# Two-layer HGRN2 + RWKV-7 trunk: 40 more projection products ahead of the inverse's corner products, gate tiles emptied by ScalarE alone, up-projection products over 128 rows

## The chip, the cores and the metric

The kernel runs on one core of one Trainium2 chip. The metric is the device time of one execution in microseconds (us), the median of three runs. One more execution was profiled; all rows of a trace below are of that one. Engines: PE is TensorE (PEld its weight loads), DVE is VectorE, ACT is ScalarE, POOL is GpSimd, SP issues most transfers.

## The reference

Two layers over a sequence of 512 with width 1024. In each layer:

```
h = x * (1 + scale) + shift            # shift, scale, gate from silu(c) @ w_ada + b_ada
P = h @ w_in                           # 49 column tiles of 128: q, f, i, z_hg | r, k, v, z_rw, w_down, a_down | g_hg, g_rw
o_hg = HGRN2(q, f, i), 4 heads of 128; normed, times silu(z_hg)
r, k, v, z_rw, w_down, a_down = token_shift(P_rw, mu)     # p + (previous token's p - p) * mu
decay from tanh(w_down) @ w_up + w0 ; a = sigmoid(a_down @ a_up + a0)
S_t = S_{t-1} (diag(w_t) - kk_t^T (a_t kk_t)) + v_t^T k_t ; y_t = S_t r_t   # RWKV-7, 8 heads of 64
y_rw = (groupnorm(y) + bonus) * silu(z_rw)
merged = sigmoid(g_hg) * (o_hg @ W_A) + sigmoid(g_rw) * (y_rw @ W_B)
x = LayerNorm(alpha * x + (1 + gate) * (merged @ w_out))
```

All is in float32.

## The kernel before

Activations lie transposed: 128 features on the partitions, 512 tokens along the free axis. A float32 product is made of three fast ones: `split` turns a weight tile into a high part (ACT copy, L120) and a low part (POOL subtraction, L125 `wl`), and `proj` (L252) multiplies high by high, high by low and low by high (L261, L262, L266). One column tile of `h @ w_in` is 24 such products of 128x512 into one PSUM tile `pj` (two of these exist), fed by two weight units of 12 products, each loaded by SP into one of three `raw` tiles and split into one of three `wh` and one of three `wl` tiles.

The recurrent part of a layer has long chains on DVE, so projection tiles serve as filling: a generator `fill` yields one product at a time, and `weave(main, fill, counts)` puts `counts[i]` of them on PE ahead of step i of `main`. Each engine works off its own queue in order, so a product that stands ahead of a step on PE is done before that step, and a step whose input is late holds everything behind it. The order of the other engines' queues comes from a scheduler that works at build time.

After the last head's preparation (p = 3) the filling is a chain of whole tiles (L1025): the merge gates `gate(j)` (two tiles each, in layer 0 one for j = 0; emptied by one ACT tanh a tile into buffers that stay until the output stage), then `zrw(p)`, then `zhg(p)`, then the other gates. A `zrw` tile ends in `rw_gate` (L666): the token shift is an ACT copy with a scale and a DVE instruction that reads PSUM (`shift`, L339: `u<-ppj,dvomm`, then L134 `u<-ppj,prm,u`), and silu is an ACT tanh and one more DVE instruction (L134 `z<-z,u`).

`rw_invert` (L501) inverts a triangular 64x64 block for each of 8 heads and 8 chunks. On DVE alone: four block transposes (L513), a substitution of many small multiplications (L125 `t<-t,t`) and sums (L521), four transposes back (L524), two more (L527). Then PE makes two sets of corner products of 32x32 (L535, copies L540 to SBUF; L549, copies L554). `WT` says how many filling products stand ahead of each quarter of these: 132 before the first, then 0, 13, 0, 14, 3, 0, 0. Ahead of them 35 (`WPR`) and 41 (`WHN`) products are taken from the same chain. Then come 8 chunks (`rw_chunk`, first instruction L577) with 24 filling products each (`WCH`), then `finish` with 65 (`WFI`), and `run(fill)` empties what is left of the chain: 57 products in layer 0 (552 in all) and 81 in layer 1 (576). Behind it come `gate_rows`, in layer 0 the `w_ada` columns of layer 1 (L302), and the branch and output projections.

`rw_wa` (L359) makes the up-projections: for each p and each of decay and a, one product over 128 rows (high weights by `x[i]`, whose halves hold the high and the low part of the activation) and one over 64 rows (low weights by the high half), L377 and L378, emptied by one ACT tanh. `wunit` splits their two weight tiles like all others. The tiles `x[i]` are of the tag `z` (four buffers), which the `w_ada` transfers of the next step need.

Of the kernel before, what the change touches and what calls it, by code (L numbers as in the profile page):

```python
# [12 lines left out]
F32 = mybir.dt.float32  # L13
F32R = mybir.dt.float32r
U8 = mybir.dt.uint8
AF = mybir.ActivationFunctionType
ALU = mybir.AluOpType
# [9 lines left out]
WHG = (0, 4, 16, 6, 11, 6, 6, 0, 8, 0, 6, 12)  # L27
WPR = (0, 4, 26, 5)
WHN = (0, 19, 0, 11, 11)
WT = (132, 0, 13, 0, 14, 3, 0, 0)  # L30
WCH = (0, 3, 3, 1, 7, 5, 5)
WNT = (0, 0, 2, 4, 0, 1, 0, 0)
WBO = (0, 31, 0, 23, 0, 18, 5, 50)
# [2 lines left out]
NP = 4  # L36
KT = 8
# [44 lines left out]
def body(ctx, tc, d):  # L82
    nc = tc.nc
    V, A, G, PE = nc.vector, nc.scalar, nc.gpsimd, nc.tensor
# [10 lines left out]
    def st(tag, shape, dt=F32):  # L95
        cnt[0] += 1
        return sp.tile(shape, dt, tag=tag, name=f"{tag}_{cnt[0]}", bufs=BUFS[tag])

    def ps(tag):
        cnt[0] += 1  # L100
        return pp.tile([128, 512], F32, tag=tag, name=f"p{tag}_{cnt[0]}", bufs=PB[tag])

    def u(shape=(128, 512), dt=F32):
        return st("u", list(shape), dt)
# [13 lines left out]
    def act(out, in_, f, scale=1.0, bias=0.0):  # L118
        if f == AF.Copy:
            A.activation(out, in_, f, scale=scale)  # L120
        else:
            A.activation(out, in_, f, scale=scale, bias=bias)  # L122

    def tt(e, o, a, b, op):
        e.tensor_tensor(o, a, b, op=op)  # L125
# [7 lines left out]
    def stt(o, a, s, b, op0, op1):  # L133
        V.scalar_tensor_tensor(o, a, s, b, op0=op0, op1=op1)  # L134
# [7 lines left out]
    mm = PE.matmul  # L142
# [54 lines left out]
    def P(n, l, i=None, w=None):  # L197
        o = PO[n, l]
        if i is not None:
            return prm[:, o + i:o + i + 1]  # L200
        return prm[:, o:o + w]

    dv = [dict() for _ in range(L)]
# [36 lines left out]
    def split(raw, hi, lo):  # L240
        act(hi, raw, AF.Copy)
        tt(G, lo, raw, hi.bitcast(F32), ALU.subtract)

    def wunit(src, th="wh", tl="wl"):
        raw = st("raw", [128, 512])
        nc.sync.dma_start(raw, src)
        hi = st(th, [128, 512], F32R)
        lo = st(tl, [128, 512], F32R)
        split(raw, hi, lo)
        return hi, lo  # L250
# [18 lines left out]
    def run(g):  # L269

        while True:
            try:
                next(g)
            except StopIteration as e:
                return e.value

    def weave(main, fill, counts, priority=0):


        last = None  # L280
        for i in itertools.count():
            for m in itertools.islice(fill, counts[i] if i < len(counts) else 0):
                last = m
            with ExitStack() as es:
                if priority:
                    es.enter_context(tc.high_priority(offset=priority))
                if last is not None:
                    es.enter_context(tc.issue_after(last.ins))
                if next(main, END) is END:
                    return  # L290
# [22 lines left out]
    def ada_next(*groups):  # L313

        for g, w in pend:
            ada_col(*g, w)
        pend[:] = []
        for l, n, k in groups:
            w = [st("z", [128, 512]) for _ in range(2)]
            for h in range(2):  # L320
                nc.sync.dma_start(w[h], d["w_ada"][l, n, k, :, h * 512:(h + 1) * 512])
            pend.append(((l, n, k), w))
# [16 lines left out]
    def shift(o, pst, l, c):  # L339
        act(o, pst, AF.Identity, scale=dv[l]["omm"][:, c:c + 1])  # L340
        stt(o[:, 1:], pst[:, :-1], P("mu", l, c), o[:, 1:], ALU.mult, ALU.add)
# [17 lines left out]
    def rw_wa(l, pst):  # L359

        wad = u()
        shift(wad, pst, l, 16)
        act(wad[0:64], wad[0:64], AF.Tanh)
        x = [st("z", [128, 512], F32R) for _ in range(2)]
        for i in range(2):
            r, q = slice(64 * i, 64 * i + 64), slice(64 - 64 * i, 128 - 64 * i)
            V.tensor_copy(x[i][r], wad[r])
            tt(V, x[i][q], wad[r], x[i][r].bitcast(F32), ALU.subtract)
        wu = [wunit(d["up"][l, i], *(("X", "X") if l else ("pu", "pu"))) for i in range(2)]
        rw["gt"], rw["vm"] = [], []  # L370
        for p in range(NP):
            cols = slice(p * 128, (p + 1) * 128)
            g = st("t4" if p < 3 else "G", [128, 2, 512])
            for i, bias in ((0, "w0"), (1, "a0")):
                r = slice(64 * i, 64 * i + 64)
                pw = ps("rw")
                mm(pw, wu[i][0][:, cols], x[i], start=True, stop=False)  # L377
                mm(pw, wu[i][1][r, cols], x[i][r], start=False, stop=True)  # L378
                act(g[:, i], pw, AF.Tanh, scale=0.5, bias=P(bias, l, p))
            rw["gt"].append(g)  # L380

# [274 lines left out]
    def silu2(z, pst):  # L656

        act(z, pst, AF.Tanh, scale=0.5)
        stt(z, z, 1.0, pst, ALU.add, ALU.mult)
        return z  # L660
# [3 lines left out]
        tt(e, o[:, 1], y, o[:, 0].bitcast(F32), ALU.subtract)  # L664

    def rw_gate(l, p, pz):  # L666
        zs = u()
        shift(zs, pz, l, 12 + p)
        return silu2(st("z", [128, 512]), zs)

    def rw_final(l, p, z, o):
        pT = ps("rw")
# [135 lines left out]
    def hg_norm(l, oT):  # L808
        act(rms, rms, AF.Sqrt, scale=1.0 / 128, bias=CRMS)
        V.reciprocal(rms, rms)  # L810
        for hd in range(NP):
            o3 = oT[hd].rearrange("p (c j) -> p c j", j=128)
            mul(G, o3, o3, bc(rms[:, hd], 128))
            yield
            pT = ps("hg")
            for t in range(4):
                PE.transpose(pT[:, t * 128:(t + 1) * 128], oT[hd][:, t * 128:(t + 1) * 128], ident)
            act(oT[hd], pT, AF.Identity, scale=P("hg", l, hd))

    def hg_gate(oT, pz):  # L820
        mul(G, oT, oT, silu2(u(), pz))
# [135 lines left out]
    for l in range(L):  # L957
        tag_h, tag_r = ("A", "B") if l == 0 else ("B", "A")
        xh = lambda kt: (hT[kt][:, 0], hT[kt][:, 1])
        ct = lambda c: proj([w_in[l, c, 0], w_in[l, c, 1]], xh)  # L960
        rw_begin(l, tag_r)
        rw_wa(l, fout[0])
        if l == 1:
            rw_vmix(l, fout[1])
# [7 lines left out]
        def late_pair(j, dt=F32):  # L972
            if j > 4:
                g = st("t4", [128, 2, 512], dt)
                return g[:, 0], g[:, 1]
            tag = ("hl", "hl", "pr", "pu", "pu")[j]
            return st(tag, [128, 512], dt), st(tag, [128, 512], dt)
# [3 lines left out]
        def gate(j):  # L981
            g = late_pair(j)
            if l == 0 and j == 0:
                g = gh0, g[0]
            else:
                o = yield from ct(CT_GH + j)
                act(g[0], o, AF.Tanh, scale=0.5)
            o = yield from ct(CT_GR + j)
            act(g[1], o, AF.Tanh, scale=0.5)
            gates.append(g)  # L990

        def zhg(hd):
            o = yield from ct(CT_ZH + hd)
            hg_gate(oT[hd], o)

        def zrw(p):
            o = yield from ct(CT_ZR + p)
            zr.append(rw_gate(l, p, o))

        def tiles(cs, outs):  # L1000
            for c in cs:
                outs.append((yield from ct(c)))
# [6 lines left out]
        for p in range(NP):  # L1009
            fill = tiles([c + p for c in (CT_R, CT_K, CT_V)][len(rkv):], rkv)  # L1010
            pi, pq, pf = hgp
            early = []
            if l == 0 and p == 0:
                fill = itertools.chain(fill, tiles([CT_I + 1], early))
            weave(hg_head(l, p, pf, pq, pi, oT), fill, WHZ if l == 0 and p == 0 else WHG)
            run(fill)
            ada_next(*itertools.islice(ada, (WAZ, WAO)[l][2 * p]))
            if p == 0:
                rw["vtm"] = [st("X", [128, 512]) for _ in range(8)]
            hgp = early  # L1020
            if p < 3:
                fill = tiles([c + p + 1 for c in (CT_I, CT_Q, CT_F)][len(hgp):], hgp)
            else:
                fill = itertools.chain.from_iterable(
                    [gate(j) for j in range(4)] + [zrw(p) for p in range(NP)] + [zhg(p) for p in range(NP)] +  # L1025
                    [gate(j) for j in range(4, KT)])
            weave(rw_prep(l, p, *rkv), fill, WPR)
            ada_next(*itertools.islice(ada, (WAZ, WAO)[l][2 * p + 1]))
            if p < 3:
                run(fill)  # L1030
            rkv = []
# [4 lines left out]
        weave(hg_norm(l, oT), fill, WHN)  # L1036
        weave(inv, fill, WT)
        for c in range(8):
# [286 lines left out]
```

## Time and profile before

| | |
|---|---|
| median of 3 runs | 1059.21 us (1058.15 to 1061.35) |
| profiled execution, its own time | 1054.03 us |
| span of that execution | 1052.2 us |
| PE busy | 961.1 us (91%) |
| DVE, POOL, ACT busy | 707.2, 564.1, 451.5 us |
| mean granted clock of TensorE | 0.965 |
| chain that ended last | PE 43%, DVE 39%, POOL 5%, issue 5%, DMA 4%, ACT 3% |

The span is the time that the trace covers; the 1.8 us between it and the execution's own time lie around it. The page gives the busy share in 40 slices of 26.3 us: PE stands at 7 to 9 tenths nearly everywhere, and the granted clock is at 9 tenths or more in all slices but the twelfth (5 tenths) and the thirty-first (7 tenths). These are the two stretches in which `rw_invert` ends.

### The profile page before, as it was taken

The numbers are of one execution on the slowest core, as the hardware profiler recorded it, in microseconds if no ns is written. First come the engines' busy times: TensorE is split into PE (matmuls) and PEld (weight loads), VectorE is DVE, ScalarE is ACT, GpSimd is POOL, SyncE is SP. The second block draws the span as 40 slices with busy tenths as digits, with TensorE's granted clock in tenths as the row PEclk, the third lists the DMA queues.
The fourth block names the chain that finished last, engine by engine and source line by source line (L and its number), as shares of the span: only waits on it lengthen the run. The fifth ranks groups of instructions, "written<-read, shape, count | busy, mean of one in ns | idle before, by whom it ended". The sixth has DMA issues, their size and how long they took to land.

```text
span 1052.2 us, 16689 instructions
## 1 busy us (share of the span) xinstructions
PE 961.1 (91%) x6132; PEld 764.9 (73%) x6132; DVE 707.2 (67%) x1259; ACT 451.5 (43%) x912; POOL 564.1 (54%) x490
## 2 busy tenths in 40 slices
PE   7988898989869999979999898988996999999997
PEld 3657687878747778857887677777885777777876
DVE  7789978478974444495675967676799544382347
ACT  3465455546314335423356445445641433534331
POOL 5464545445414557767544554545552456576765
PEclk9999999999959999999999999999997999999999
DMA  8834532313301112574544422222131111345422
GB/s 304 293 101 137 173 102 60 91 53 88 98 17 48 52 52 79 171 232 141 169 144 138 132 82 62 80 80 62 59 101 50 52 52 49 93 150 160 121 81 80
DMA packets 61748, 112.83 MB, mean 107 GB/s; under 512 B 6865, under 2 KB 11361, under 8 KB 61666
## 3 DMA queue, kind: packets, MB, share of 16 engines
q1 hardware_dynamic: 57778, 105.12, 32.4%
q10 hardware_dynamic: 3888, 6.64, 2.1%
q8 instruction: 48, 0.79, 0.3%
q14 instruction: 34, 0.28, 0.1%
HBM read 106.49 MB, written 5.25 MB: 106 GB/s over the span
## 4 chain that ended last, share of the span: by engine, by line
PE 43%; DVE 39%; POOL 5%; issue 5%; DMA 4%; ACT 3%; SPq 0%; POOLq 0%; DVEq 0%; ACTq 0%
PE ppj L262 9%; PE ppj L261 9%; PE ppj L266 8%; DVE t L125 4%; DVE z L302 4%; POOL wl L125 3%; DVE t L521 3%; DVE hl L125 3%; DVE u L125 2%; DVE B L302 2%; DMA z<-in_w_ada 2%; DVE t L513 2%; DVE ar L524 2%; PE prw L577 2%; DVE u L131 1%
## 5 line engine op out<-in xcount | busy, mean ns | idle before, releaser
L125 POOL TENSOR_TENSOR wl<-raw,wh 128x512 fp32r<-128x512 f32 (+1 forms) x233 | 318.2, 1370 | 284.0 <-ACT wh L120 158.0
L120 ACT ACTIVATE wh<-raw 128x512 fp32r<-128x512 f32 (+1 forms) x233 | 144.3, 623 | 143.6 <-PE ppj L262 90.6
L261 PE MATMUL ppj<-B,wh 128*128 128x512 f32 x432 | 175.5, 406 | 7.5 <-ACT wh L120 5.9
L262 PE MATMUL ppj<-B,wh 128*128 128x512 f32 x432 | 175.0, 405 | 0.0
L261 PE MATMUL ppj<-A,wh 128*128 128x512 f32 x400 | 165.8, 414 | 6.2 <-DVE u L134 6.0
L262 PE MATMUL ppj<-A,wh 128*128 128x512 f32 x400 | 165.3, 413 | 0.0
L266 PE MATMUL ppj<-B,wl 128*128 128x512 f32 x432 | 123.4, 401 | 1.2 <-POOL wl L125 1.2
L266 PE MATMUL ppj<-A,wl 128*128 128x512 f32 x400 | 115.8, 405 | 2.0 <-POOL wl L125 2.0
L261 PEld LDWEIGHTS ppj<-B,wh 128*128 128x128 f32 x432 | 83.0, 192 | 25.7 <-ACT wh L120 8.0
L262 PEld LDWEIGHTS ppj<-B,wh 128*128 128x128 f32 x432 | 82.9, 192 | 16.5
L261 PEld LDWEIGHTS ppj<-A,wh 128*128 128x128 f32 x400 | 78.3, 196 | 22.8 <-DVE u L134 4.2
L266 PEld LDWEIGHTS ppj<-B,wl 128*128 128x128 f32 x432 | 80.2, 190 | 19.6 <-POOL wl L125 3.3
L262 PEld LDWEIGHTS ppj<-A,wh 128*128 128x128 f32 x400 | 78.5, 196 | 15.8 <-issue 0.2
L266 PEld LDWEIGHTS ppj<-A,wl 128*128 128x128 f32 x400 | 75.6, 193 | 19.0 <-POOL wl L125 3.3
L125 POOL TENSOR_TENSOR hl<-hl,u 128x256 f32<-128x256 f32 x40 | 34.2, 855 | 42.9 <-DVE u L748 20.5
L125 DVE TENSOR_TENSOR t<-t,t 128x144 f32<-128x144 f32 (+29 forms) x62 | 42.6, 688 | 2.1
L753 PE MATMUL phg<-u 128*128 128x128 f32 x160 | 28.7, 308 | 16.1 <-DVE hl L755 13.7
L753 PEld LDWEIGHTS phg<-u 128*128 128x128 f32 x160 | 24.8, 209 | 24.3 <-ACT u L762 14.8
L131 DVE TENSOR_SCALAR u<-u,dvh 128x512 f32<-128x512 f32 x8 | 7.5, 939 | 43.3 <-ACT u L122 43.3
L302 DVE CUSTOM_DVE_ANT_0 z<-z,mbd,prm 128x512 f32<-128x512 f32 x32 | 29.9, 936 | 8.7 <-DMA z<-in_w_ada 8.4
L125 DVE TENSOR_TENSOR W<-prw,d 64x256 f32<-64x256 f32 x32 | 13.5, 422 | 29.4 <-PE prw L601 28.9
L125 DVE TENSOR_TENSOR hl<-hl,u 128x256 f32<-128x256 f32 x64 | 31.6, 513 | 0.5
(470 smaller groups left out, 1963.2 us busy)
## 6 DMA issues: line engine op xcount, KB each, us to landing
raw<-in_w_in SPq DMA_DIRECT2D x182, 256.0 KB, 2.6
z<-in_w_ada SPq DMA_DIRECT2D x64, 256.0 KB, 3.4
B<-in_w_ada SPq DMA_DIRECT2D x16, 512.0 KB, 6.1
raw<-in_w_br SPq DMA_DIRECT2D x32, 256.0 KB, 2.7
raw<-in_w_out SPq DMA_DIRECT2D x32, 256.0 KB, 2.7
u<-in_x SPq DMA_DIRECT2D x8, 256.0 KB, 4.2
o<-in_w_in SPq DMA_DIRECT2D x14, 128.0 KB, 4.2
t<-in_xt SPq DMA_DIRECT2D x6, 256.0 KB, 3.3
```

Of the source, the lines that this page charges most:

```text
L120: A.activation(out, in_, f, scale=scale)
L125: e.tensor_tensor(o, a, b, op=op)
L131: e.tensor_scalar(o, a, s1, s2, op0=op0, op1=op1)
L261: yield mm(o, w, xh, start=half == 0 and k == 0, stop=False)
L262: yield mm(o, w, xl, start=False, stop=False)
L266: yield mm(o, w, xh, start=False, stop=half == n - 1 and k == 3)
L302: V.tensor_tensor_reduce(out=w[h], in0=w[h], in1=silc[h], scale=0.5, scalar=0.0 if h else init, op0=ALU.mult, op1=ALU.add, accum_out=part[ ...
L513: V.transpose(Tin[qs].rearrange("p t s -> p s t"), ax[qs, :, cs_].rearrange("p h s -> p s h"))
L521: V.tensor_reduce(blk(R, t, [32, j]), pv, axis=AX.X, op=ALU.add)
L524: V.transpose(ax[qs, :, cs_].rearrange("p h t -> p t h"), R[qs].rearrange("p j t -> p t j"))
L577: mm(pg[h][:, p * 128:(p + 1) * 128], BK[p][hs, ch], ZR[p][hs, ch], start=p == 0, stop=p == 3)
L753: mm(pS[:, c * 128:(c + 1) * 128], kp[:, c * 128:(c + 1) * 128], ql[:, c * 128:(c + 1) * 128], start=c == 0, stop=c == 1)
```

## The change

`WT` begins with 172 in place of 132, so 40 more filling products stand ahead of the first corner products in each layer. The chain of filling tiles has five gates ahead of the `zrw` tiles, where it had four. `rw_gate` empties its PSUM tile by two ACT copies, adds them on POOL, and leaves DVE one instruction that reads SBUF alone. In `rw_wa` the unused half of the low weights is set to zero on POOL, and the second product runs over all 128 rows.

```diff
-WT = (132, 0, 13, 0, 14, 3, 0, 0)
+WT = (172, 0, 13, 0, 14, 3, 0, 0)
...
         wu = [wunit(d["up"][l, i], *(("X", "X") if l else ("pu", "pu"))) for i in range(2)]
+        for i in range(2):
+
+            G.memset(wu[i][1][64 - 64 * i:128 - 64 * i].bitcast(F32), 0.0)
...
             for i, bias in ((0, "w0"), (1, "a0")):
-                r = slice(64 * i, 64 * i + 64)
                 pw = ps("rw")
                 mm(pw, wu[i][0][:, cols], x[i], start=True, stop=False)
-                mm(pw, wu[i][1][r, cols], x[i][r], start=False, stop=True)
+                mm(pw, wu[i][1][:, cols], x[i], start=False, stop=True)
                 act(g[:, i], pw, AF.Tanh, scale=0.5, bias=P(bias, l, p))
...
     def rw_gate(l, p, pz):
-        zs = u()
-        shift(zs, pz, l, 12 + p)
-        return silu2(st("z", [128, 512]), zs)
+        z, t = st("z", [128, 512]), u()
+        act(z, pz, AF.Identity, scale=dv[l]["omm"][:, 12 + p:13 + p])
+        act(t[:, 1:], pz[:, :-1], AF.Identity, scale=P("mu", l, 12 + p))
+        tt(G, z[:, 1:], z[:, 1:], t[:, 1:], ALU.add)
+        act(t, z, AF.Tanh, scale=0.5)
+        stt(z, t, 1.0, z, ALU.add, ALU.mult)
+        return z
...
-                    [gate(j) for j in range(4)] + [zrw(p) for p in range(NP)] + [zhg(p) for p in range(NP)] +
-                    [gate(j) for j in range(4, KT)])
+                    [gate(j) for j in range(5)] + [zrw(p) for p in range(NP)] + [zhg(p) for p in range(NP)] +
+                    [gate(j) for j in range(5, KT)])
```

## Rows read from the trace of the kernel before

**Rows 1.** Windows: stretch, its length, each engine's busy time, granted clock, DMA share.

```profile
290.00:306.00 16.00, 7.02 (x75) 5.33 (x76) 15.10 (x10) 0.63 (x1) 0.00 (x0) 0.50 0.01 1
318.00:406.00 88.00, 88.00 (x906) 67.74 (x906) 39.56 (x74) 34.12 (x67) 47.71 (x46) 1.00 0.18 49
406.00:436.00 30.00, 30.00 (x142) 24.82 (x141) 9.08 (x12) 15.08 (x25) 23.53 (x18) 1.00 0.41 126
```

**Rows 2.** Timeline of PE, layer 0's inverse: start, duration, instruction, idle before.

```profile
285.54 0.39 PE L261 MATMUL ppj<-A,wh 128*128 128x512 f32 x1
...
286.22 0.39 PE L262 MATMUL ppj<-A,wh 128*128 128x512 f32 x1
293.62 0.31 PE L535 MATMUL prw<-ar 32*32 32x32 f32 x2 [7.01 <-DVE ar L524]
295.82 1.92 PE L535 MATMUL prw<-ar 32*32 32x32 f32 x62 [1.89 <-DVE ar L524]
...
304.91 0.80 PE L261 MATMUL ppj<-A,wh 128*128 128x512 f32 x1 [3.46 <-DVE u L134]
...
318.69 1.16 PE L577 MATMUL prw<-B,B 64*128 64x128 f32 x16
```

**Rows 3.** Timeline of DVE, layer 0's inverse.

```profile
282.76 0.59 DVE L125 TENSOR_TENSOR t<-t,t 128x416 f32<-128x416 f32 x1
...
284.01 0.96 DVE L125 TENSOR_TENSOR t<-t,t 128x432 f32<-128x432 f32 x1
...
291.40 8.82 DVE L524 STREAM_TRANSPOSE ar<-t 32x1024 f32<-32x1024 f32 x4
300.24 3.84 DVE L527 STREAM_TRANSPOSE t<-t 32x1024 f32<-32x1024 f32 x2
304.11 0.75 DVE L134 SCALAR_TENSOR_TENSOR u<-ppj,prm,u 128x511 f32<-128x511 f32 x1
```

**Rows 4.** Timeline of ACT, layer 0's inverse.

```profile
283.02 0.69 ACT L122 ACTIVATE u<-ppj,dvomm 128x512 f32<-128x512 f32 x1 [0.23 <-PE ppj L266]
...
304.89 0.63 ACT L122 ACTIVATE z<-u 128x512 f32<-128x512 f32 x1 [19.38 <-DVE u L134]
```

**Rows 5.** Timeline of POOL, layer 0's inverse.

```profile
283.12 1.38 POOL L125 TENSOR_TENSOR wl<-raw,wh 128x512 fp32r<-128x512 f32 x1 [1.43 <-PE ppj L266]
```

**Rows 6.** Timeline of PE, layer 1's inverse.

```profile
798.77 0.39 PE L262 MATMUL ppj<-B,wh 128*128 128x512 f32 x1
806.18 0.31 PE L535 MATMUL prw<-ar 32*32 32x32 f32 x2 [7.02 <-DVE ar L524]
...
824.87 1.16 PE L577 MATMUL prw<-A,A 64*128 64x128 f32 x16
```

**Rows 7.** Timeline of DVE, layer 1's inverse.

```profile
803.96 8.82 DVE L524 STREAM_TRANSPOSE ar<-t 32x1024 f32<-32x1024 f32 x4
...
816.76 0.68 DVE L540 COPY t<-prw 32x512 f32<-32x512 f32 x1
```

**Rows 8.** Timeline of PE, layer 1's up-projections (L377, L378) and what follows.

```profile
559.93 0.39 PE L377 MATMUL prw<-z,X 128*128 128x512 f32 x1
...
566.27 0.79 PE L378 MATMUL prw<-z,X 64*128 64x512 f32 x1
...
570.14 0.39 PE L396 MATMUL prw<-z,z 128*128 128x512 f32 x1
```

**Rows 9.** Windows, the end of layer 1's up-projections.

```profile
566.00:568.00 2.00, 2.00 (x4) 1.14 (x5) 0.00 (x0) 1.49 (x3) 0.62 (x1) 0.55 0.41 130
```

**Rows 10.** Chain that ended last, behind them: start, duration, what.

```profile
571.42 5.06 DMA z<-in_w_ada
```

**Rows 11.** One line of the code, the zeroing of a 128x512 tile: ns min/median/max.

```profile
L1033 POOL MEMSET mbd<- x2: 527/529/531, 141.9 to 606.0; 128x512 f32 x2
```

**Rows 12.** Timeline of PE, layer 1's remaining filling after the chunks.

```profile
943.41 0.50 PE L261 MATMUL ppj<-B,wh 128*128 128x512 f32 x1 [1.20 <-ACT t L122]
```

**Rows 13.** Timeline of DVE, the first gated sum of layer 1's output stage.

```profile
952.35 0.69 DVE L134 SCALAR_TENSOR_TENSOR u<-hl,ppj 128x512 f32<-128x512 f32 x1 [5.33 <-PE ppj L266]
```

## The prediction

> **What bounds the kernel now.** The page comes first: PE is busy for 91% of the span, so a gain must come from stretches in which PE waits or runs slowly. The granted clock by slices shows two such places, one in each layer. The windows then say how bad they are: between 290 and 306 us PE has 7.02 us of work in 16, at a clock of 0.50 (1.2 of 2.4 GHz), while DVE is busy for 15.10 of 16; before and after, PE is full at 1.00 [rows 1]. The timelines of the engines give the order of events in layer 0. The 132nd filling product starts at 286.22; products follow each other by 0.227 us (three starts from 285.54 to 286.22), so PE is free at 286.45. The corner products need two of DVE's four transposes back, which begin at 291.40: PE idles 7.01 us, does two records, idles 1.89 more, and goes on at 295.82 at half clock [rows 2, 3]. It then stops for 3.46 us because a filling tile waits for a DVE instruction. ACT shows why: the first `zrw` tile was finished at 283, its shift on DVE stands behind all transposes and runs at 304.11, and ACT's tanh behind it waited 19.38 us, with every weight split behind it [rows 3, 4]. Only at 318.69 does the first chunk begin [rows 2]. Layer 1 has the same 7.02 us wait and begins its chunks at 824.87 [rows 6]. After that PE is full: 88.00 of 88 us in layer 0's chunks, 30.00 of 30 behind them [rows 1]. What PE does earlier there shortens the layer.
>
> **The change part by part.**
>
> *40 more products.* They cost 40 x 0.227 = 9.1 us of PE, in a hole of 7.01 + 1.89 = 8.9 us, and are missing from the filling that is left behind the chunks (57 and 81 products). The totals stay, so each layer's last filling is 9.1 us shorter: 18.2 us together. Their 3.3 weight units are loaded and split earlier too; the DMA share in the hole is 0.01 and POOL is at 0.00 of 16 us [rows 1], so SP's transfers and the splits are hidden. Exposed, they would be up to 1.38 us a unit on POOL [rows 5].
>
> *The inverse, layer 0.* From 286.45 the 40 products last to 295.5. DVE gets slower: multiplications that meet a split on POOL take longer (0.96 us at 284.01 against 0.59 for nearly the same size at 282.76, the split began at 283.12) [rows 3, 5]. Two more splits fall among DVE's last multiplications; I take 0.6 us in all, between nothing and 2.8 (two whole splits). The transposes then begin at 292.0, two of them (8.82/4 = 2.2 us each) end at 296.4, and the corner products start there. A half of them took 1.92 us at half clock [rows 2]; PE no longer rests for long, so I expect full clock and take 1.1 us, between 0.96 and 1.92. Then 13 products to 300.4, the second half to 301.5, 14 products to 304.7. DVE ends the other transposes at 292.0 + 8.82 + 3.84 = 304.7 and makes its copy (0.68 us, as in layer 1 [rows 7]), ACT a second one of like length: 306.0. The second set, 2.2 us and 3 products, ends at 308.9. The first chunk began at 318.69: 9.8 us gained. The 3.46 us stall goes because no PSUM tile waits for DVE any more; DVE's last instruction on z holds only SBUF buffers (one of six `u`, one of four `z`), for which nobody queues yet.
>
> *The inverse, layer 1.* The fill ends at 799.0 + 9.1 = 808.1, the two transposes at 803.96 + 0.6 + 4.4 = 809.0; corner, 13 products, corner, 14 products: 817.3. The copies begin at 816.76 + 0.6 and end at 818.7; the second set and 3 products end at 821.6 against 824.87: 3.3 us [rows 6, 7]. This layer had not the ACT stall on a `zrw` tile, so it has less to give back.
>
> *`rw_gate`.* Each of 8 tiles gets one more ACT copy (0.69 us [rows 4]) and a POOL addition (a split of the same size takes 1.38 us [rows 5]), and loses one DVE instruction of 0.75 [rows 3]. ACT's tanh now waits for POOL; queued behind it are weight splits and, in the chunks, the copies that the next chunk step needs. With 278 products ahead of the chunks and 24 in each, tiles now end 10 products into a chunk, where they ended 2 (layer 0: 238 before). That is beside the corrected-value products. In the chunks ACT has 34.12 and POOL 47.71 of 88 us of work [rows 1], so I charge 1.5 us for both layers, between a gain of 1 and a loss of 5. A fifth gate ahead costs nothing: its tiles are emptied by ACT as before, into `pu` buffers that the last head has left by then.
>
> *Up-projections.* In layer 1, the products of 128 and of 64 rows follow each other by 0.42 us (15 steps from 559.93 to 566.27), PE is busy throughout, and the clock falls to 0.55 at their end; by 570.14 PE has done 25 products in 10.4 us [rows 8, 9]. At 0.227 us each they would take 5.7: at most 4.7 us. Each pair must be emptied by ACT; twelve tiles at 0.69 us are 8.3 us, which leaves about 2.2. The chain goes on through the `w_ada` transfer that needs these `z` buffers [rows 10], so it is on the path. I take 3.5, between 0 and 4.7. The Trainium skill ("TensorE: Matmul & The Clock Gate", step-by-step part on LDWEIGHTS) says that loading time follows the columns and that the row count doesn't matter; by that the 64-row products would cost no more than the others and this edit would give 0, 3.5 us less in the sum. The rows speak against it. The two zeroings are 0.53 us each [rows 11], on POOL between its splits and ahead of a product that waits for DVE anyway: 0, at worst 1.1 a layer. In layer 0 DVE's head chain runs beside the up-projections; I take 0, between -1 and 1.
>
> *Behind the chunks.* Not all there is filling. In layer 0 POOL has 23.53 us of work in 30 [rows 1]; without 3.3 splits it has about 19 in 21, so I charge 1 us (0 to 4). In layer 1 DVE's residual rows hang on transfers that begin when the last `z` tiles are read, a fixed time after the chunks. They ended at 952.35 - 5.33 = 947.0, and ACT, which waits for them too, already cost PE 1.20 us at 943.4 [rows 12, 13]. With PE 9.1 us earlier against them, the 5.33 us of DVE's slack is gone and some 3.8 are missing. DVE's order may change; I charge 3 us, between 0 and 9.
>
> *Sum.* 9.8 + 3.3 + 18.2 + 3.5 - 1.5 - 1 - 3 = 29.3 us. Against the profiled execution's 1054.0: 1024.7. The median of the runs lies 5.2 us above that execution, so the median becomes 1030.
>
> **Rivals.** (a) *The ends don't shrink.* What follows the chunks is pinned to them by POOL and DVE, not by filling: layer 1 loses 9 and layer 0 4. For it: the 1.20 us wait and POOL's load; against it: PE is full there. Gain 20, time 1039. (b) *The hole moves.* ACT and POOL, in order, hold the splits of the 40 products or the copies between the corner sets, and PE idles and slows down there after all: the 13.1 us of the inverse don't come. Time 1043. (c) *POOL holds DVE.* Every DVE multiplication with POOL beside it waits to POOL's end: 2.8 us in place of 0.6 a layer, and in the output stages alike. Time 1034, inside my range. The Trainium skill ("SBUF — State Buffer", who interferes with whom) has such a rule: a DVE instruction with two SBUF inputs and a POOL one that reads SBUF block each other fully. (d) *Rows don't matter*, the rule above as a mechanism: the second edit is hidden by ACT. Time 1033.5. (e) *Slower.* Tiles that end 10 products into a chunk put ACT's and POOL's new work between a chunk's corrected values and its state product, and each of 16 chunks gets longer. It takes 29.3/16 = 1.8 us a chunk to eat the gain; at 2.5 us the time is 1070. Against it: all of `rw_gate`'s new work is 0.69 + 1.4 us, in 5 chunks of 16. (f) *No net change*: several of these sum to the gain; 1059.
>
> **How the numbers follow.** The forecast (1022 to 1037) has 0.66, (a) 0.16, (b) 0.06, (d) as far as it is not in the forecast 0.04, (f) 0.03, (e) 0.05. Best case: 13.1 + 18.2 + 4.7 without losses, 36 us, 1023. The range goes from 1022 to 1044, to hold (a), (c) and (d) and most of (b). About 0.3% is what a measurement of this kernel can tell from no change; faster by more 0.92, within 0.03, slower 0.05.
>
> **What would show it.** Right: no idle time of several us on PE at L535, clock 1.00 through both inverses, the first L577 of layer 0 about 10 us sooner and that of layer 1 about 3 us sooner, counted from their own transposes L524; ACT without a 19 us wait; L377 and L378 0.23 us apart; `run(fill)` 9 us shorter. Wrong: L577 periods over 11.0 us (88/8 [rows 1]), PE waits for ACT behind layer 1's chunks beyond 5 us, or L540 copies held on ACT while PE stands.

## The result, and the profile after

The changed kernel takes 1032.02 us (median of 4 runs, 1030.67 to 1033.58) against 1060.28 (4 runs beside it, 1058.15 to 1062.19): ratio 0.9734, 95% interval 0.9707 to 0.9762. The forecast was 1030 us, with a range from 1022 to 1044. The profiled execution took 1030.67 us with a span of 1028.9. Comparisons leave disturbed executions out (one of before beside the experiments, and the profiled one of `e8_up1`).

The page of after, busy time and granted clock by slices: PE is busy for 93% of the span, and both dips of before, to 5 and to 7 tenths, are gone.

```profile
PE 951.9 (93%) x6132; PEld 761.9 (74%) x6132; DVE 700.1 (68%) x1251; ACT 454.3 (44%) x920; POOL 578.9 (56%) x502
...
PEclk9989899999999999999999999999999999998999
```

Windows of after, with the columns of [rows 1] (`PEld` busy time stands behind PE's, the last three columns are granted clock, DMA share and GB/s); the first is the hole, the others are layer 0's chunks and the rest of its filling. In the hole PE now works 14.67 us of 16 at full clock, where it worked 7.02 at half; POOL works beside DVE, 8.26 us where it did nothing.

```profile
290.00:306.00 16.00, 14.67 (x181) 11.84 (x180) 15.76 (x10) 3.79 (x7) 8.26 (x7) 1.00 0.28 81
312.91:398.30 85.39, 84.48 (x878) 64.73 (x877) 37.31 (x72) 33.86 (x67) 49.59 (x47) 1.00 0.17 48
398.30:420.80 22.50, 22.50 (x122) 18.53 (x121) 12.54 (x14) 12.90 (x21) 16.95 (x14) 1.00 0.40 119
```

Timeline of PE in layer 0's inverse (after [rows 2]; lines up to `rw_gate` are 2 higher than before). The 7.01 us wait is gone, and half a set of corner products takes 1.19 us in place of 1.92. What is left are waits of 1.33, 1.11 and 0.36 us. Three filling products, the first chunk's own, follow the last corner products (L551), and the first chunk begins at 312.91 in place of 318.69; in it PE waits 0.91 us for ACT's copy to `ar` (L556), and the second chunk follows after 11.38 us.

```profile
296.65 0.24 PE L537 MATMUL prw<-ar 32*32 32x32 f32 x2
298.23 1.19 PE L537 MATMUL prw<-ar 32*32 32x32 f32 x62 [1.33 <-DVE ar L526]
...
302.56 1.20 PE L537 MATMUL prw<-ar 32*32 32x32 f32 x64
...
308.27 0.24 PE L551 MATMUL prw<-t,t 32*32 32x32 f32 x2 [1.11 <-DVE t L542]
308.88 0.69 PE L551 MATMUL prw<-t,t 32*32 32x32 f32 x30 [0.36 <-ACT t L542]
...
310.39 1.71 PE L551 MATMUL prw<-t,t 32*32 32x32 f32 x96
312.02 0.50 PE L261 MATMUL ppj<-A,wh 128*128 128x512 f32 x1
312.36 0.40 PE L262 MATMUL ppj<-A,wh 128*128 128x512 f32 x1
312.59 0.39 PE L261 MATMUL ppj<-A,wh 128*128 128x512 f32 x1
312.91 1.16 PE L579 MATMUL prw<-B,B 64*128 64x128 f32 x16
...
315.89 0.33 PE L591 MATMUL prw<-cc,W 128*128 128x128 f32 x1 [0.91 <-ACT ar L556]
...
324.29 1.16 PE L579 MATMUL prw<-B,B 64*128 64x128 f32 x16
```

Timeline of DVE there (after [rows 3]). Two instructions `z<-u,z`, the last step of the new `rw_gate`, stand in front of the copies L542 and L556. The second waits 4.74 us for ACT's tanh while the copies to `ar` queue behind it.

```profile
289.67 1.74 DVE L125 TENSOR_TENSOR t<-t,t 128x480 f32<-128x480 f32 x1
291.44 0.66 DVE L523 TENSOR_REDUCE t<-t 128x16 f32<-128x480 f32 x1
...
293.55 9.28 DVE L526 STREAM_TRANSPOSE ar<-t 32x1024 f32<-32x1024 f32 x4
302.84 4.06 DVE L529 STREAM_TRANSPOSE t<-t 32x1024 f32<-32x1024 f32 x2
306.93 0.69 DVE L134 SCALAR_TENSOR_TENSOR z<-u,z 128x512 f32<-128x512 f32 x1
307.54 1.27 DVE L542 COPY t<-prw 32x512 f32<-32x512 f32 x2
313.55 1.08 DVE L134 SCALAR_TENSOR_TENSOR z<-u,z 128x512 f32<-128x512 f32 x1 [4.74 <-ACT u L122]
314.56 1.27 DVE L556 COPY ar<-prw 32x512 f32<-32x512 f32 x2
```

Timeline of ACT (after [rows 4]): the 19.38 us wait is gone; the longest is now 9.49, ahead of the first L542 copy. Between ACT's two copies a weight split and the emptying of a z tile are queued, but PE did not wait for the second one: PE has no idle time from 308.88 to the first chunk.

```profile
308.25 0.58 ACT L542 COPY t<-prw 32x512 f32<-32x512 f32 x1 [9.49 <-DVE t L542]
308.85 0.63 ACT L120 ACTIVATE wh<-raw 128x512 fp32r<-128x512 f32 x1
309.50 0.69 ACT L122 ACTIVATE z<-ppj,dvomm 128x512 f32<-128x512 f32 x1
310.22 0.58 ACT L542 COPY t<-prw 32x512 f32<-32x512 f32 x1
```

Timeline of PE in layer 1's up-projection (L379 and L380 are L377 and L378 of before): products of 128 rows follow each other by 0.23 us, and from the first of them to the last row shown it is 5.7 us, where it was 10.2 [rows 8].

```profile
546.48 0.40 PE L379 MATMUL prw<-z,X 128*128 128x512 f32 x1
546.71 0.40 PE L380 MATMUL prw<-z,X 128*128 128x512 f32 x1
...
552.20 0.40 PE L398 MATMUL prw<-z,z 128*128 128x512 f32 x1
```

Timelines of the weight loads (PEld) there, with one product of PE in between; first before, then after:

```profile
560.25 0.18 PEld L378 LDWEIGHTS prw<-z,X 64*128 64x128 f32 x1 [0.24 <-issue]
560.25 0.49 PE L378 MATMUL prw<-z,X 64*128 64x512 f32 x1
560.67 0.19 PEld L377 LDWEIGHTS prw<-z,X 128*128 128x128 f32 x1 [0.24 <-DVE z L389]
```
```profile
546.48 0.19 PEld L380 LDWEIGHTS prw<-z,X 128*128 128x128 f32 x1
546.71 0.19 PEld L379 LDWEIGHTS prw<-z,X 128*128 128x128 f32 x1
```

A load takes the same time for 64 and for 128 rows. Before, a product's load starts at the product's own start (560.25), and PEld idles for 0.24 us ahead of it; after, the load for the product at 546.71 stands at 546.48, beside the product before it.

Layer 1's output stage: PE waits 3.66 us for ACT where it waited 1.20 [rows 12] (first fence), and DVE's first gated sum has lost its 5.33 us of slack [rows 13] (second).

```profile
927.97 0.50 PE L261 MATMUL ppj<-A,wh 128*128 128x512 f32 x1 [3.66 <-ACT t L122]
```
```profile
929.70 0.67 DVE L134 SCALAR_TENSOR_TENSOR u<-hl,ppj 128x512 f32<-128x512 f32 x1
```

Stages, worked out as differences of the starts of marked instructions in the timelines of each profiled execution (us; the experiments follow below):

| stage | before | after | e2_fill | e3_gate | e5_quiet | e7_192 | e10_best |
|---|---|---|---|---|---|---|---|
| start to layer 0's transposes | 245.75 | 246.79 | 250.87 | 251.02 | 244.45 | 246.12 | 244.78 |
| transposes to first chunk, layer 0 | 72.94 | 66.12 | 69.03 | 69.31 | 62.73 | 67.26 | 67.27 |
| chunks, layer 0 | 84.21 | 85.39 | 84.20 | 85.08 | 84.57 | 88.04 | 84.20 |
| rest of filling, layer 0 | 31.41 | 22.47 | 22.48 | 31.41 | 22.48 | 17.79 | 17.79 |
| to layer 1's up-projection | 125.62 | 125.71 | 126.70 | 125.51 | 127.41 | 130.15 | 129.78 |
| to layer 1's transposes | 198.37 | 195.61 | 199.97 | 201.10 | 194.22 | 195.66 | 193.42 |
| transposes to first chunk, layer 1 | 66.57 | 65.48 | 65.44 | 68.01 | 62.73 | 67.26 | 67.26 |
| chunks, layer 1 | 85.35 | 86.31 | 85.12 | 86.62 | 85.88 | 86.82 | 85.12 |
| to the first output product | 50.10 | 44.00 | 45.08 | 50.09 | 43.96 | 42.08 | 41.10 |
| to the end | 91.88 | 91.02 | 88.91 | 89.15 | 89.57 | 86.52 | 87.68 |

Before to after these are -23.3 us together, while the medians differ by 28.3. The profiled execution of before (1054.03) was quicker than most: in 40 executions of before beside the experiments the time goes from 1049.8 us at a mean granted clock of 0.969 to 1065.8 at 0.953 (correlation -0.88), with a median of 1056.9. 16 executions of the changed kernel (after and two later repeats of it, `e6_defer` and `e12_ctl`) lie between 1028.5 and 1034.6 at 0.973 to 0.986, with a median of 1031.1: 26 us less.

What makes before's times spread stays open. The profiles do not show that the time at low clock behind a hole differs: with both holes, before and `e1_up` have a granted clock of 0.64 and 0.61 from 310 to 315 us, 1.00 from 315 to 320, and 0.96 and 0.94 from 815 to 820. The up-projection is a rival. `e1_up`, which has the holes but products of 128 rows, spreads over 6.9 us in ten executions, where before beside it spreads over 14.8 in 19; `e11_up1b`, without the holes but with 64-row products in layer 0, spreads over 11.5 in six.

### The profile page after: what moved, and what is told of

Same layout as the page of the kernel before. It is cut to its first block, busy times and chain, and to the rows that moved or that the text cites. A ratio compares the mean times of both kernels' runs of the same rounds, so it can differ in the third digit from the quotient of the medians.

```text
span 1028.9 us, 16689 instructions
## 1 busy us (share of the span) xinstructions
PE 951.9 (93%) x6132; PEld 761.9 (74%) x6132; DVE 700.1 (68%) x1251; ACT 454.3 (44%) x920; POOL 578.9 (56%) x502
## 4 chain that ended last, share of the span: by engine, by line
PE 44%; DVE 40%; issue 6%; POOL 5%; DMA 3%; ACT 2%; POOLq 0%; DVEq 0%; ACTq 0%; SPq 0%
PE ppj L266 9%; PE ppj L261 9%; PE ppj L262 9%; DVE t L125 4%; DVE z L302 4%; DVE hl L125 3%; DVE t L523 3%; POOL wl L125 3%; DVE u L125 2%; DVE B L302 2%; DVE ar L526 2%; DVE t L515 2%; DVE u L134 1%; PE prw L579 1%; DMA z<-in_w_ada 1%
## 5 line engine op out<-in xcount | busy, mean ns | idle before, releaser
L261 PE MATMUL ppj<-B,wh 128*128 128x512 f32 x432 | 174.4, 404 | 4.5 <-ACT wh L120 3.9
L262 PE MATMUL ppj<-B,wh 128*128 128x512 f32 x432 | 172.4, 399 | 0.0
L261 PE MATMUL ppj<-A,wh 128*128 128x512 f32 x400 | 164.1, 410 | 5.6 <-ACT t L122 3.7
L262 PE MATMUL ppj<-A,wh 128*128 128x512 f32 x400 | 162.7, 407 | 0.0
L266 PE MATMUL ppj<-B,wl 128*128 128x512 f32 x432 | 126.0, 403 | 2.1 <-POOL wl L125 2.1
L266 PE MATMUL ppj<-A,wl 128*128 128x512 f32 x400 | 117.9, 407 | 1.7 <-POOL wl L125 1.6
L125 DVE TENSOR_TENSOR t<-t,t 128x144 f32<-128x144 f32 (+29 forms) x62 | 44.8, 723 | 2.1
L125 DVE TENSOR_TENSOR raw<-raw,X 128x512 f32<-128x512 f32 x8 | 5.9, 742 | 38.5 <-DMA raw<-in_w_out 31.9
```

Source lines behind the costliest of these rows:

```text
L261: yield mm(o, w, xh, start=half == 0 and k == 0, stop=False)
L262: yield mm(o, w, xl, start=False, stop=False)
L266: yield mm(o, w, xh, start=False, stop=half == n - 1 and k == 3)
```

## The experiments

**Each edit by itself.** `e1_up` is before with the up-projection edit alone, `e2_fill` with the 172 products and five gates alone, `e3_gate` with the new `rw_gate` alone; `e4_noup` is the changed kernel without the up-projection edit.

```
# e2_fill, e4_noup:
-WT = (132, ...
+WT = (172, ...
+[gate(j) for j in range(5)] + ...
# e3_gate, e4_noup: the new rw_gate, as in the change
# e1_up:
+G.memset(...)
+mm(pw, wu[i][1][:, cols], x[i], ...)
```

> The kernel before with only the up-projection products over 128 rows (and their zeroings). Theory (each edit acts in its own stage and the sums add): layer 1's stretch gains 2 to 3 us, layer 0's start loses 1 us as in the trace after, so 1 to 2.5 us faster than before, ratio 0.998 to 0.999. Rival (row count does not matter): products still 0.42 us apart, ratio 1.000.

> The kernel before with only the 40 products more and the fifth gate ahead; the zrw tiles still go through DVE. Theory A (the moved products are most of the gain, whoever empties the tiles): in layer 0 the first zrw tile ends only 8 products ahead of the corner products, ACT is blocked by DVE for some 10 us behind it, PE stalls 2 to 5 us after the corner products; layer 1 loses nothing; ratio 0.975 to 0.982. Rival B (ACT alone emptying the tiles is what lets the products move): the block on ACT starves the splits, PE idles as long as before and the ratio stays above 0.988.

> The kernel before with only the new emptying of zrw tiles (ACT, ACT, POOL, ACT, DVE), 132 products and four gates as before. Theory A: the idle time of 8.9 us ahead of the corner products stays in both layers; only layer 0's 3.5 us stall and some half-clock time go, ratio 0.994 to 0.998. Rival B: most of the gain, ratio below 0.988.

> The changed kernel with the up-projection as before. Theory (sums add): 1 to 2.5 us slower than the changed kernel, ratio to before 0.974 to 0.976. Rival (the faster start of layer 1 is lost again before its inverse): the same as the changed kernel, 0.973.

Medians beside before's 1056.63: `e1_up` 1053.17 (ratio 0.9974, 0.9946 to 1.0002), `e2_fill` 1037.71 (0.981, 0.9764 to 0.9856), `e3_gate` 1056.41 (1.0005, 0.9966 to 1.0044), `e4_noup` 1036.33 (0.9809, 0.977 to 0.9847). The moved products, with the fifth gate (not tried apart from them), carry most of the gain, 18.9 us. The single gains sum to 22.6 of some 26 us. The expectation for `e2_fill` held, stall included. `e1_up` was to give 1 to 2.5 us and gave 3.5, though its interval just holds no change; `e4_noup` was to lose 1 to 2.5 us and lies 5.3 above the median of the 16 executions of the changed kernel, none of which ran beside it. `e3_gate` was to give 0.2 to 0.6% and missed: the new `rw_gate` alone gives nothing that can be measured. Its inverse in layer 0 is 3.6 us shorter than before's, but the chunks of the two layers are longer by 0.9 and 1.3. Its place in the whole is seen in `e2_fill`, which keeps the shift on DVE. Timelines of its PE and of its ACT, at the old stall:

```profile
311.56 0.50 PE L261 MATMUL ppj<-A,wh 128*128 128x512 f32 x1 [2.85 <-DVE u L134]
```
```profile
311.54 0.63 ACT L122 ACTIVATE z<-u 128x512 f32<-128x512 f32 x1 [11.82 <-DVE u L134]
```

So the 40 products alone leave 2.85 of the 3.46 us stall [rows 2], and layer 0's inverse at 69.03 in place of 66.12; but their chunks, 84.20 and 85.12, are the shortest. `rw_gate` takes 2.9 us out of layer 0's inverse and puts 1.2 into the first chunk of each layer (its period is 10.19 us in `e2_fill` and 11.38 in after).

**POOL beside DVE.** `e5_quiet` is the changed kernel in which the gate tiles ahead of the corner products and the first three z tiles use the rounded part of their weights in place of the small remainder too, so that POOL has no splits there.

```
...
+        act(hi, raw, AF.Copy)
+        return hi, hi
...
```

> Changed kernel, but the weights of the gate tiles ahead of the corner products and of the first three z tiles keep their rounded part only (the small remainder is not computed, the rounded part stands in its place), so POOL has 1.3 us a split less beside DVE's substitution. Theory A (POOL's splits slow DVE down): the substitution of layer 0, 46.8 us from its first transposes to the next ones, falls to 40 us or less, the transposes behind it from 9.3 to 8.9 us, and PE's wait ahead of the corner products goes negative, so the inverse to the first chunk shortens from 66.1 to 62 us or less and the median falls 5 to 12 us below the changed kernel's 1032. Theory B (DVE's time there is its own, POOL beside it costs under 1 us): 46 us, inverse within 1 us of 66.1, median within 3 us.

Median 1023.38 (ratio 0.9666, 0.9626 to 0.9706), 6.7 us below the changed kernel beside it (1030.08, `e6_defer`): theory A, although the inverse of layer 0 stayed at 62.73 us, a little above the 62 expected. Windows over DVE's substitution, `e5_quiet` and then after, with POOL's busy time ahead of the last three columns:

```profile
244.45:282.00 37.55, 37.55 (x175) 31.12 (x175) 35.36 (x66) 15.83 (x32) 0.09 (x1) 1.00 0.32 91
```
```profile
246.80:293.50 46.70, 46.70 (x215) 38.72 (x215) 44.52 (x66) 19.26 (x36) 24.72 (x20) 1.00 0.34 96
```

The same 66 DVE instructions take 9.2 us less when POOL is silent. What gets shorter are the multiplications, which read two SBUF tiles; the reductions don't change. The one of 128x480 took 1.74 us in after and 0.66 here, the reduction behind it 0.66 and 0.65:

```profile
279.22 0.66 DVE L125 TENSOR_TENSOR t<-t,t 128x480 f32<-128x480 f32 x1
279.92 0.65 DVE L530 TENSOR_REDUCE t<-t 128x16 f32<-128x480 f32 x1
...
282.02 9.43 DVE L533 STREAM_TRANSPOSE ar<-t 32x1024 f32<-32x1024 f32 x4
```

The transposes, 9.43 against 9.28, were not POOL's doing; expecting 8.9 was wrong. In `e5_quiet` POOL did nothing at all during these 9.43 us. They take 8.82 or 8.83 us in the three profiles with a hole there (before, `e1_up`, `e3_gate`) and 9.1 to 9.4 in the ten others. In before PE worked 4.71 us of the 8.82 at half clock, ACT nothing, and the DMA share was 0.01; in `e5_quiet` they were 9.43 at full clock, 3.20 and 0.32. No run tells these apart. With POOL silent PE has no wait in the corner products: DVE is done before the 172 products.

**The last multiplication of a z tile.** `e6_defer` issued it behind the third chunk in the program's order.

```
...
+            if c == 2:
+                flush()            # stt(z, t, 1.0, z, ...) of the first two z tiles
...
```

> Changed kernel, but DVE's last multiplication of the first two z tiles of each layer is issued behind the third chunk. Theory A (this multiplication, which waits 4.7 us for ACT's tanh and POOL's sum, stands ahead of the inverse's last copies and of the first chunk's mask): the first chunk's period falls from 11.4 to 10.3 us, the first chunk of layer 0 starts up to 1 us earlier, 1.5 to 3 us less together, median 1029 to 1031. Theory B (DVE is held there by the copies' own inputs): no stage changes by over 0.5 us.

It tested nothing: the scheduler put the instruction back, and on every engine the order is that of the changed kernel. So its 1030.08 us (ratio 0.9726, 0.9689 to 0.9762) are a control. `e9_late` holds the instruction back behind DVE's state update of that chunk.

```
...
+        with tc.issue_after(rw["aV"].ins):      # aV: the last tensor_tensor into mbd
+            for z, t in rw["late"]:
+                stt(z, t, 1.0, z, ALU.add, ALU.mult)
...
```

> Changed kernel, with DVE's last multiplication of the first three z tiles of each layer now really queued behind the third chunk's state update (each held back behind that instruction on DVE; an earlier attempt left DVE's order as it was). Theory A (this multiplication, waiting 4.7 us for ACT's tanh, stands ahead of the inverse's last copies to `ar` and so sets the first chunk's py products): the first chunk's period falls from 11.4 to 10.6 us or less in both layers, PE's 0.9 us wait for ACT's `ar` copy goes, 1.5 to 3 us together in the stages from the inverse to the chunks' end. Theory B (the copies wait for PE's corner products anyway): first period within 0.3 us of 11.38.

> The changed kernel itself, as a control in the same call: 1029 to 1033 us, ratio 0.971 to 0.976.

1028.40 us (ratio 0.9717, 0.9683 to 0.9751) against 1032.84 of the control beside it, `e12_ctl` (0.9755, 0.9721 to 0.979). The first chunk's period, counted from L579 to L579, is 10.19 us in both layers, against 11.38 in after and 11.89 and 11.35 in the control; the other periods are 11.08 to 11.09 in all. The chunks take 84.20 and, in layer 1, 85.12 again, as in `e2_fill`, and PE's wait for the `ar` copy is gone. Timeline of PE in `e9_late`, to be read beside 312.91 and 324.29 of after:

```profile
312.69 1.16 PE L579 MATMUL prw<-B,B 64*128 64x128 f32 x16
...
322.88 1.16 PE L579 MATMUL prw<-B,B 64*128 64x128 f32 x16
```

This is theory A. The two first periods give 2.4 us, inside the 1.5 to 3 expected. The 4.4 us between the medians are not all from there: the control is the same program as after and `e6_defer`, whose medians are 1032.02 and 1030.08, and in its profile the granted clock fell to 0.50 from 310 to 315 us, at the end of layer 0's inverse, where after's stood at 1.00. Against the 16 executions together `e9_late` is 2.7 us faster.

**More products.** `e7_192` has 192 products ahead of the corner products; `e10_best` has them too and holds back both the tanh and the last multiplication of three z tiles.

> Changed kernel with 192 products in place of 172 ahead of the corner products. Theory A (products beyond the hole only move: 20 x 0.227 = 4.5 us longer to the first chunk, 4.5 shorter behind the chunks): median within 3 us of the changed kernel; layer 0's inverse 69 to 71 us. Theory B (what follows the chunks no longer shortens, because DVE, POOL and transfers pin layer 1's end): the tails shrink by under 2.5 us each, the median rises by 4 to 9 us. Theory C (DVE still holds PE at 172): the inverse grows by under 2 us and the median falls by 4 us or more.

> Changed kernel with 192 products ahead of the corner products, and both the tanh and the last multiplication of the first three z tiles queued behind the third chunk (tanh on ACT, multiplication on DVE). With 192 alone the first chunk's period was 14.0 us in layer 0, of which PE waited 2.15 us for ACT's `ar` copy, which stood behind a tanh that waited 3.6 us for POOL. Theory A (those waits are the only price of the 20 products): first period 10.6 us or less, inverse as with 192 alone (67.3 us), so 4 to 6 us below the changed kernel, median 0.4 to 0.6% lower than its control in this job. Theory B (the 20 products come back elsewhere, as they did in layer 1's tail): within 2 us of the control.

`e7_192`: 1028.79 us (ratio 0.9717, 0.968 to 0.9753), 1.3 below its control, inside their spreads. Against after, its layer 0 spends 1.14 us more in the inverse and 2.65 more in the chunks, and 4.4 more on the way to layer 1's up-projection, and gets 4.7 back in the filling. The median fits A, but the inverse does not: it grew by 1.14 us where A had 3 to 5, since PE has no more waits for DVE in the corner products, as in C. What the 20 products meet is the first chunk, 14.03 us long, on PE:

```profile
317.59 1.11 PE L591 MATMUL prw<-cc,W 128*128 128x128 f32 x4 [2.15 <-ACT ar L556]
```

and on the timeline of its DVE the z tile that waits for ACT, ahead of the copies:

```profile
315.64 0.69 DVE L134 SCALAR_TENSOR_TENSOR z<-u,z 128x512 f32<-128x512 f32 x1 [6.75 <-ACT u L122]
316.25 1.27 DVE L556 COPY ar<-prw 32x512 f32<-32x512 f32 x2
```

In `e10_best` nothing of z stands there, and the copies wait for PE alone:

```profile
305.03 1.28 DVE L542 COPY t<-prw 32x512 f32<-32x512 f32 x2
310.26 0.68 DVE L556 COPY ar<-prw 32x512 f32<-32x512 f32 x1 [3.95 <-PE prw L551]
311.27 0.68 DVE L556 COPY ar<-prw 32x512 f32<-32x512 f32 x1 [0.33 <-PE prw L551]
```

Its window of the hole, with PE full:

```profile
290.00:306.00 16.00, 16.00 (x188) 13.04 (x187) 15.76 (x11) 4.69 (x8) 8.01 (x6) 1.00 0.29 82
```

1022.08 us (1020.18 to 1023.88; ratio 0.9663, 0.9627 to 0.9698) against the control's 1029.5 to 1034.6: 10.8 us or 1.0% below the changed kernel (9.0 below the median of its 16 executions), and the first period is 10.19. This is the fastest version with the whole computation. More than theory A's 4 to 6 came: against the control's profile layer 1 gives more behind its chunks than the 4.5 us of products (2.9 + 3.7 against the control's 43.98 and 91.35) and 2.7 us ahead of its transposes (193.42 against 196.07), which I had not foreseen and did not take apart. Of layer 0's 4.7, 3.2 come back before layer 1's up-projection (129.78 against the control's 126.58); PE's waits there, most of them for ACT and POOL, add up to 11.6 us against 9.8, and the rest stays open. `e7_192` and `e9_late` together hold all of this edit but the later tanh, which was not tried by itself.

**Layer 0's up-projection.** `e8_up1` and, as a repeat, `e11_up1b` have the 128-row products in layer 1 alone.

```
+        r = slice(0, 128) if l else slice(64 * i, 64 * i + 64)
+        mm(pw, wu[i][1][r, cols], x[i][r], start=False, stop=True)
```

> Changed kernel with the 128-row up-projection products in layer 1 only; layer 0 as before the change. Theory A (layer 0's zeroing and longer products cost as much as they give there, since DVE's head chain sets the pace): layer 0 up to its first transposes 245.7 against 246.8, median within 1.5 us of the changed kernel. Theory B (the edit works in layer 0 too): 1 us or more later in layer 0, median 1033 or more.

> The changed kernel with the 128-row up-projection products in layer 1 only, again, since the profiled execution of the first run of it was disturbed. Theory A (in layer 0 the edit gives nothing, DVE's head chain sets the pace): median within 1.5 us of the control. Theory B (it pays in layer 0 too, as the first run's 1037 against 1030 says): 3 to 8 us above the control, and layer 0 up to its first transposes longer by that much.

1035.41 us (ratio 0.9783, 0.9739 to 0.9826; five executions from 1033.4 to 1039.5) against 1030.08, and then 1032.74 (0.9757, 0.9715 to 0.9799; 1026.8 to 1038.3) against 1032.84: once theory B, once A. (The 1037 in the second expectation counts a sixth execution, of 4793 us.) The traces show two cases of the same code. Windows of `e2_fill`, whose layer 0 also has the 64-row products, and of after:

```profile
70.00:80.00 10.00, 10.00 (x21) 5.00 (x20) 5.50 (x14) 3.94 (x9) 2.77 (x4) 0.50 0.13 38
```
```profile
70.00:80.00 10.00, 8.48 (x39) 6.63 (x39) 9.15 (x18) 6.92 (x15) 6.01 (x7) 0.87 0.26 85
```

With the 64-row products the clock in this window was 0.50 in two profiles (`e2_fill`, `e3_gate`), which then reach the transposes at 250.9 and 251.0, and 1.00 in three (before, `e4_noup`, `e11_up1b`), at 243.9 to 245.8. With 128 rows it was 0.84 to 1.00 in all eight, at 244.5 to 247.2. So in layer 0 the edit costs about 1 us where the clock holds and saves about 5 where it does not; how often that is, and what makes the clock fall in some executions, stays open.

## Why the prediction was right, point by point

| term | foreseen | profiled pair |
|---|---|---|
| inverse, layer 0 | 9.8 | 6.8 |
| inverse, layer 1 | 3.3 | 1.1 |
| filling less what pins it (18.2 - 1 - 3) | 14.2 | 15.9 (8.9 + 7.0) |
| up-projection, layer 1 | 3.5 | 2.8 |
| `rw_gate`, chunks | -1.5 | -2.1 |
| layer 0's start and the way to layer 1 | 0 | -1.1 |
| sum | 29.3 | 23.3 |

The mechanism was right: the hole, the clock and the stall went, and the filling came off both ends. Rivals (a) and (f) fall with it, and of (b) only the waits of 1.11 and 0.36 us for the copies were there, in layer 0. That the median came out 2 us from the forecast is in part luck, as two errors met. The sum was 6.0 us too large: it put the profiled execution at 1024.7, and that took 1030.67. The 5.2 us added to it, the distance of before's median from its profiled execution, were 1.4 for the changed kernel.

Of the signs, the wait at L535, the clock of this execution, ACT's wait, the 0.23 us and layer 0's filling came as said. Counted from their transposes back, the first chunks came 7.9 and 2.2 us sooner, where 10 and 3 were said. The sign "periods over 11.0 us" could not tell: before's own periods are 10.19 and then 11.08 to 11.09.

*The inverse* is where it was mis-sized: 3.0 us in layer 0, set on the start's 1.04 us delay, and 2.2 in layer 1. In layer 0 the transposes ended 1.2 us later than I had: POOL cost DVE 1.1 us in the substitution (46.76 against 45.65), where I took 0.6, and the transposes themselves took 9.28 + 4.06 against 8.82 + 3.84, where I took no change. The z multiplication ahead of L542 took 0.69, which I had not counted. From the end of ACT's first copy to the first chunk it was 4.1 us, where I had 2.9: the first chunk puts three filling products ahead of its own first instruction (`WCH` begins with 0, 3), 0.9 us that my sum left out, and the second set took 0.3 more. That is 3.1 us together. Layer 1 has no z multiplication there; its transposes ended 1.0 us late, and the last 1.2 us are the same as in layer 0.

The sentence that fell is that for DVE's last instruction on z "nobody queues yet": no one waits for z, but DVE's own next instructions queue behind it. Its price is the 0.69 us here and 1.2 in each first chunk, which `e9_late` gives back.

*rw_gate.* The charge of 1.5 us was about right in size and wrong in place. I put it at tiles that end 10 products into a chunk; the six later periods did not move (11.09), which speaks against rival (e), and all of it is in the first chunk, through the copies of L556.

*Up-projection.* Over all profiles the stretch from layer 1's up-projection to its transposes is 193.4 to 197.6 us in nine with the edit (mean 195.6) and 198.4 to 202.8 in four without (mean 200.6): 5.0 us. The two groups differ in the other edits too, and single pairs give from 0.8 (before and `e1_up`) to 7.2 (`e4_noup` and after), so the size of what arrives stays open. The 16 products themselves, to the next instruction of another line, take 3.8 us in all nine and 6.8 to 8.6 in the four, and rival (d) falls. My upper bound was off by a misreading: the stretch of [rows 8] is 570.14 - 559.93 = 10.2 us and not 10.4, so the bound is 4.5. The Trainium skill ("TensorE: Matmul & The Clock Gate", step-by-step part on LDWEIGHTS) has loading time depend on columns and not on rows. The trace agrees for the load itself, 0.18 us for 64 rows and 0.19 for 128. A price of nothing for the step does not follow: the pairs of 128 and 64 rows stand 0.42 us apart [rows 8], against 0.23 of 128 rows alone. By the rows of PEld above, the load then no longer lies beside the product before it; that its 0.18 us make the difference of 0.19 is inferred, not tested.

*Rival (c)* was right as a mechanism and wrong as a price of this change. POOL holds 9.2 us of DVE's substitution in after, but most of that was there before, and the change added 1.1. The Trainium skill ("SBUF — State Buffer", who interferes with whom) says that a DVE instruction with two SBUF inputs and a POOL one block each other; `e5_quiet` agrees, 1.74 against 0.66 us, with reductions untouched. After's POOL shows the other direction: two of its splits that began during such a multiplication (286.88 and 292.32) took 1.58 and 1.63 us, where most took 1.29.

*Behind the chunks.* Layer 1's first output product came 6.1 us sooner, which is the 9.1 less the 3 that I charged, and the waits stood where [rows 12, 13] said. Layer 0's charge of 1 us did not come: 8.94 of 9.1.

## What to carry to other kernels

When a wait is taken off one engine by handing its tile to others, look at what stands behind the tile's last instruction on every engine that still touches it: here 1 us of DVE's work, waiting for ACT and POOL, held the copies that the next stage begins with; queueing it later gave 2.4 us in the first chunks, and with the tanh queued later too, 20 further products pay (1022.08 against 1028.40 us). A hole in PE costs its length and the low clock behind it. Executions of one kernel can differ by more than half of what a change gives (16 us in 40 executions of before, against 26), so size a gain from several runs and not from one profile, and do not carry over a distance between profile and median. When you add up a path to an instruction, count the filling that stands directly ahead of it. And after issuing something later, read the engine's real order before trusting the time.

## What the runs showed of the hardware

POOL's 1.3 us subtractions stretch DVE's multiplications of two SBUF tiles (0.66 to 1.74 us for 128x480) and leave its reductions (0.65 and 0.66) and its transposes (9.43 and 9.28 for four) alone; over a substitution of 66 instructions that is 37.55 against 46.70 us. Weight loads of 64 and of 128 rows take 0.18 and 0.19 us, but products that alternate between the two follow each other by 0.42 us and those of 128 rows alone by 0.23. In layer 0 the same 64-row products ran at a granted clock of 1.00 in three profiles and at 0.50, with PE busy for 10.00 of 10 us, in two.
